# Two adaLN columns ahead of x, squares summed on TensorE, h from wide products, angles and softplus on GpSimd

## The chip, the core and the metric

The kernel runs on one core of a Trainium2 chip. The metric is the device time of one execution in microseconds (us); lower is better. TensorE (PE) multiplies matrices into PSUM; its weight loads stand apart as PEld. VectorE (DVE), ScalarE (ACT) and GpSimd (POOL) do the elementwise work, SyncE (SP) issues most of the transfers. Each engine takes its instructions from a queue of its own, in order, and waits on semaphores for the others.

## The reference

A decoder trunk of two layers on one sequence of 256 tokens, 1024 wide. Each layer modulates a normalised x by the condition c (adaLN), projects it once for three branches, and adds the gated merge to x. Cut to what matters here:

```python
c_act = jax.nn.silu(c)
mod = c_act @ ada_w + ada_b                      # 3072 columns a layer
shift, scale, gate = jnp.split(mod, 3, axis=-1)
h = rmsnorm(x, norm_g) * (1.0 + scale) + shift   # 256 x 1024
z = h @ w_in                                     # 1024 x 13312, split into:
# a_x, a_g | b_q, b_k, b_v, b_g | c_q, c_k, c_v, c_g | m_g
# A: u = causal_dwconv(a_x); log_a = -8 * sigmoid(..u..) * softplus(-lam); scan; * silu(a_g)
# B: q = rope(rmsnorm(b_q, qn_g), pos) / 8; k = rope(rmsnorm(b_k, kn_g), pos); attention; * silu(b_g)
# C: log_alpha from (h @ gla_a1) @ gla_a2; chunked linear attention; * silu(c_g)
x = x + gate * ((mg0 * (ya @ proj_a) + mg1 * (yb @ proj_b) + mg2 * (yc @ proj_c)) @ w_o)
```

`rope` turns q and k by the cosine and sine of the angle position times inverse frequency. Softplus of lam concerns 1024 numbers a layer, and only branch A's gates use it.

## The kernel before, in words

**Layout.** x lies with its 1024 features on 8 x 128 partitions and the 256 tokens along the free axis (`x_sb`, 128 x 8 x 256). All weights come as one stream (`ws`) in units, in an order fixed in the program. A unit is a piece of a projection: T units are 256 rows of the matrices q, k, v or bg with up to 512 columns (four of them make one matrix for one pair of heads), F units 128 columns over all 1024 rows (conv branch `ax`, its gate `ag`, and others). SyncE loads each unit into one of six `raw` buffers. Matmuls run in three products to keep f32 accuracy: ScalarE casts `raw` to `whi` (L232), VectorE takes the remainder `wlo` (L233), and TensorE adds hi·hi, lo·hi and hi·lo (L799 to L801 for q, k, v and others of their kind, L787 to L789 for bg, L807 to L809 for F units). There are four `whi` and four `wlo` buffers, and four PSUM buffers `mm`.

**adaLN.** c is activated, and `crow` is made of it by matmuls of ones with a diagonal (L318, L322): c's 1024 numbers along the free axis, on every partition. A column of the modulation is then one product with sum on VectorE (`ada_tile`, L334), over 1024 elements per partition. Layer 0 needs 16 columns, a scale and a shift for each of the 8 tiles of h; a scale is multiplied by the norm's weight (L336) and is then `mod`. The table `START` sets which columns stand ahead of which unit in the stream: four before unit 0, four before unit 4, and so on. The first ten are loaded into buffers that lie free at the start (`ada_yhi`, `ada_ylo`, `ada_hraw`, ...).

**The start.** SyncE issues c, the unit matrix, x in two halves, the vector of small parameters (`vec_sb`), and then the stream. `stats_start` squares x on ScalarE (L381, four instructions of 512 columns), adds the squares on VectorE (L384, L385), and sums over partitions by two matmuls with ones (L388). `rstd_full` turns this into 1/rms by ln and exp on ScalarE and one step of Newton's method on VectorE (L351 to L357). The casts of units 0 to 3 are put behind these steps by `tc.issue_after`.

**The first block.** Units 0 to 15 are q, k, v and bg of the first pair in four rounds. Between them stand the adaLN columns; with each shift column `h_tile` makes one tile of h: VectorE the product of x, `mod` and rstd (`tmp`, L366), ScalarE `hhi` (L368), VectorE `hlo` (L369). Hooks at units 2, 15 and 16 add `tables` (the angles in `angles`, their sine and cosine, and the tables `ctab` and `stab` that also hold the norm weights of q and k), loads of masks, and `small` (`softplus`, L399 to L410).

**The hand-over.** When a matrix is done, `evac_qk` squares it on ScalarE, makes two products with the tables on VectorE (`ra` L562, `rb` L564) and a sum of the squares (`ss` L566), adds the halves on GpSimd (`ro`, L567 and L568), and at its end scales `ss` and raises it to the power -1/2 on GpSimd (L569, L570). `gen_qk` multiplies `ro` by `ss` on VectorE (L575), and TensorE transposes the product (L177). q and k have two PSUM buffers each, one for each half of the tokens: q0, q1, k0, k1. The next units, the F units of the conv branch, take those buffers in turn; each of them is evacuated on VectorE by the steps of the convolution (`ya`, L887). `gen_la` runs in between: it splits the factor of the low-rank decay into `a_sb` (GpSimd, L479) and `t` (L466) and multiplies them on TensorE (L469, L485). bg's result becomes `sgb` (L858).

**What sets the order.** The program is written in the order of the dependences; a list scheduler with a time for each instruction sorts each engine's queue, and `tc.issue_after` puts an instruction behind another. A pool's buffer is waited for by whoever writes it next.

## Time and profile before

| | |
|---|---|
| three runs, us | 906.34, 906.39, 908.03 (median 906.39) |
| the profiled execution, us | 906.63, of which span 904.9 |
| TensorE busy | 865.6 us (96%), weight loads 818.7 (90%) |
| VectorE busy | 671.9 us (74%) |
| ScalarE busy | 531.8 us (59%) |
| GpSimd busy | 179.1 us (20%) |
| moved | 170.16 MB |

The span runs from the first instruction to the last of the profiled execution, and the device time holds a little around it. The shares are averages over stages that differ; the rows below take the first 100 us apart, where all that the change touches is done. In a timeline a row gives the start, the duration, the engine, the line, the operation, out<-in by the program's names with shape, and in brackets the idle time ahead of it and what ended it. Durations of neighbours can overlap, since an instruction begins while the one before it drains.

### The profile page before, as it was taken

Reading aid. Unit: us, or ns where it says so; the run is one execution under the profiler, and the core shown is the slowest. Engines: PE = TensorE matmul, PEld = TensorE weight load, DVE = VectorE, ACT = ScalarE, POOL = GpSimd, SP = SyncE. Lnnn points to the kernel's source line nnn. Section 1 sums busy time; section 2 is a strip of 40 time slices with the busy share of each in tenths; the row PEclk is TensorE's granted clock in tenths of the full one; section 3 lists DMA queues with packets and bytes.
Section 4 is the critical chain, followed back from the end, with each engine's and each line's share of the span. In section 5 each row is a group of like instructions: output and inputs, shape, how many; then the busy total and the mean of one; then the engine's idle time right before and its main releaser. Section 6 shows DMA issues by size and latency. Waiting matters only on the chain.

```text
span 904.9 us, 16407 instructions
## 1 busy us (share of the span) xinstructions
PE 865.6 (96%) x6340; PEld 818.7 (90%) x6340; DVE 671.9 (74%) x1115; ACT 531.8 (59%) x897; POOL 179.1 (20%) x160
## 2 busy tenths in 40 slices
PE   3989999999999999999999999989999999999998
PEld 2978999999988888998989999979999988899998
DVE  6998899669667667656776788986896666656674
ACT  4376976686544554644454689666874545554451
POOL 0026365224000110100030525651430001000000
PEclk7999999999999999999999999999999999999999
DMA  8884456446756666676654644553567455455651
GB/s 334 309 290 138 146 174 193 141 134 195 248 184 197 205 212 201 212 236 205 224 168 148 191 146 144 176 194 117 184 205 239 163 189 166 148 173 187 191 167 47
DMA packets 52111, 170.16 MB, mean 188 GB/s; under 512 B 6240, under 2 KB 8160, under 8 KB 52032
## 3 DMA queue, kind: packets, MB, share of 16 engines
q1 hardware_dynamic: 51216, 167.04, 56.8%
q10 hardware_dynamic: 672, 1.87, 0.7%
q8 instruction: 50, 0.82, 0.4%
q0 software_dynamic: 144, 0.20, 0.2%
q14 instruction: 29, 0.24, 0.1%
HBM read 168.23 MB, written 1.05 MB: 187 GB/s over the span
## 4 chain that ended last, share of the span: by engine, by line
PE 51%; DVE 19%; DMA 12%; issue 8%; ACT 5%; POOL 4%; DVEq 0%; SPq 0%; ACTq 0%
DMA raw<-in_ada_dram 10%; PE mm L807 10%; PE mm L809 10%; PE mm L808 10%; DVE wlo L233 8%; PE mm L799 5%; PE mm L800 5%; PE mm L801 4%; POOL ss L570 2%; PE xps L177 1%; ACT whi L232 1%; DVE raw L334 1%; DVE rb L564 1%; DMA g_raw<-in_gates_dram 1%; DVE ra L562 1%
## 5 line engine op out<-in xcount | busy, mean ns | idle before, releaser
L233 DVE TENSOR_TENSOR wlo<-raw,whi 128x1024 fp32r<-128x1024 f32 (+2 forms) x288 | 335.3, 1171 | 84.5 <-ACT whi L232 83.1
L232 ACT CAST whi<-raw 128x1024 fp32r<-128x1024 f32 (+2 forms) x288 | 280.1, 976 | 185.2 <-PE mm L808 120.4
L807 PE MATMUL mm<-hhi,whi 128*128 128x256 f32 x768 | 217.1, 283 | 2.9 <-DVE rb L564 2.9
L809 PE MATMUL mm<-hhi,wlo 128*128 128x256 f32 x768 | 216.0, 282 | 3.5 <-DVE wlo L233 3.5
L808 PE MATMUL mm<-hlo,whi 128*128 128x256 f32 x768 | 215.4, 280 | 0.0
L799 PE MATMUL mm<-whi,hhi 128*128 128x384 f32 (+2 forms) x480 | 169.5, 358 | 7.2 <-ACT hhi L368 6.5
L800 PE MATMUL mm<-wlo,hhi 128*128 128x384 f32 (+2 forms) x480 | 171.3, 358 | 1.6 <-DVE wlo L233 1.4
L801 PE MATMUL mm<-whi,hlo 128*128 128x384 f32 (+2 forms) x480 | 167.6, 355 | 0.5 <-DVE hlo L369 0.5
L807 PEld LDWEIGHTS mm<-hhi,whi 128*128 128x128 f32 x768 | 146.0, 190 | 4.5 <-ACT tmp L857 2.9
L809 PEld LDWEIGHTS mm<-hhi,wlo 128*128 128x128 f32 x768 | 145.6, 190 | 4.7 <-DVE wlo L233 4.1
L808 PEld LDWEIGHTS mm<-hlo,whi 128*128 128x128 f32 x768 | 145.7, 190 | 0.3
L799 PEld LDWEIGHTS mm<-whi,hhi 128*128 128x128 f32 x480 | 92.9, 195 | 14.5 <-ACT hhi L368 7.5
L800 PEld LDWEIGHTS mm<-wlo,hhi 128*128 128x128 f32 x480 | 93.4, 195 | 9.1 <-DVE wlo L233 3.2
L334 DVE CUSTOM_DVE_ANT_0 raw<-raw,crow,vec_sb 128x1024 f32<-128x1024 f32 x38 | 48.7, 1283 | 70.2 <-DMA raw<-in_ada_dram 70.2
L801 PEld LDWEIGHTS mm<-whi,hlo 128*128 128x128 f32 x480 | 92.5, 194 | 6.7 <-DVE hlo L369 0.8
L807 PE MATMUL mm<-yhi,whi 128*128 128x256 f32 x320 | 89.9, 281 | 1.5 <-DVE mg L949 1.5
L808 PE MATMUL mm<-ylo,whi 128*128 128x256 f32 x320 | 89.4, 279 | 0.0
L809 PE MATMUL mm<-yhi,wlo 128*128 128x256 f32 x320 | 89.2, 279 | 0.0
L807 PEld LDWEIGHTS mm<-yhi,whi 128*128 128x128 f32 x320 | 60.4, 189 | 2.5 <-DVE mg L949 1.7
L809 PEld LDWEIGHTS mm<-yhi,wlo 128*128 128x128 f32 x320 | 60.1, 188 | 0.8 <-DVE mod L334 0.4
L808 PEld LDWEIGHTS mm<-ylo,whi 128*128 128x128 f32 x320 | 60.1, 188 | 0.0
L708 POOL TENSOR_TENSOR at_hl<-att_sb,at_hl 128x384 fp32r<-128x384 f32 x8 | 8.8, 1096 | 206.3 <-ACT at_hl L707 206.3
(236 smaller groups left out, 1409.2 us busy)
## 6 DMA issues: line engine op xcount, KB each, us to landing
raw<-in_ws_dram SPq DMA_DIRECT2D x192, 512.0 KB, 4.2
raw<-in_ws_dram SPq DMA_DIRECT2D x88, 384.0 KB, 3.1
raw<-in_ada_dram SPq DMA_DIRECT2D x38, 512.0 KB, 4.5
raw<-in_ws_dram SPq DMA_DIRECT2D x8, 400.0 KB, 4.6
g_raw<-in_gates_dram ACTq DMA_DIRECT2D x3, 512.0 KB, 4.5
x_sb<-in_x_t_dram SPq DMA_DIRECT2D x2, 512.0 KB, 6.6
ada_yhi<-in_ada_dram SPq DMA_DIRECT2D x2, 512.0 KB, 7.8
ada_ylo<-in_ada_dram SPq DMA_DIRECT2D x2, 512.0 KB, 9.0
```

The costliest lines, as they stand in the source:

```text
L177: seen[0] = T.transpose(*a, **k).ins
L232: A.copy(hi, r)
L233: V.tensor_tensor(lo, r, hi.bitcast(F32), ALU.subtract)
L334: V.tensor_tensor_reduce(w, w, crow2, 1.0, b, ALU.mult, ALU.add, a if i == 0 else m)
L562: V.tensor_tensor(ra.rearrange("p (g s) d -> p g s d", g=3), z4, ctab[l][:, i, t].unsqueeze(2).to_broadcast(bc), ALU.mult)
L570: G.tensor_tensor(ss, ss, mhalf[:, 0:12].rearrange("p (a b) -> p a b", a=2), ALU.pow)
L799: T.matmul(o, ah, wh, start=(k == 0), stop=False)
L800: T.matmul(o, ah, wl, start=False, stop=False)
L801: T.matmul(o, al, wh, start=False, stop=(k == KT - 1))
L807: T.matmul(ps[:, 0:S], hi[:, a:b], xh[:, k], start=(k == 0), stop=False)
L808: T.matmul(ps[:, 0:S], hi[:, a:b], xl[:, k], start=False, stop=False)
L809: T.matmul(ps[:, 0:S], lo[:, a:b], xh[:, k], start=False, stop=(k == nk - 1))
```

## The change

- The first two adaLN columns are loaded ahead of x, and `vec_sb` on ScalarE's queue.
- At the start TensorE runs eight matmuls of ones by ones, two with the diagonal and, in `rstd_full`, three of `m`, whose results nobody reads. The squares are not added on VectorE any more: TensorE sums all eight tiles.
- h of layer 0 is made by `h_first`: VectorE multiplies x by rstd in wide pieces (`xr`, L382: 256, 256, 512 and 1024 columns), ScalarE applies scale and shift (`tmp`) and casts (`hhi`), VectorE takes the remainder (`hlo`, L393). The product of a scale with the norm's weight goes to ScalarE.
- The angles go to GpSimd but for the last limit, softplus to GpSimd but for one reciprocal, with Abs and Relu on ScalarE. In place of one fused step each, GpSimd takes two. The tables take four products in place of eight.
- The casts of units 0 to 3 are tied to other instructions, and `tables` no longer waits for the last `hlo`.

```diff
         if it in early:
...
+            if it[2] == 1:
+                for i in range(2):
+                    SY.dma_start(out=x_sb[:, 4 * i:4 * i + 4], in_=x_t[:, 4 * i:4 * i + 4])
...
                     if it[1] < 4:
-                        st.enter_context(tc.issue_after(cur["ra"]))
-                        st.enter_context(tc.issue_after(cur["rv"]))
+                        st.enter_context(tc.issue_after(cur["h0a" if it[1] else "ra"]))
                     A.copy(hi, r)
+                with ExitStack() as st:
+                    if it[1] < 4:
+                        st.enter_context(tc.issue_after(cur["xr0"]))
                     V.tensor_tensor(lo, r, hi.bitcast(F32), ALU.subtract)
...
+    A.dma_start(out=vec_sb, in_=vec)
     SY.dma_start(out=eye_sb, in_=eye)
-    for i in range(2):
-        SY.dma_start(out=x_sb[:, 4 * i:4 * i + 4], in_=x_t[:, 4 * i:4 * i + 4])
-    SY.dma_start(out=vec_sb, in_=vec)
...
+    warm_up(ones, 8)
...
+    warm_up(diag[:, 0:2].rearrange("p k n -> p (k n)"), 2)
...
         if i == 0:
-            V.tensor_tensor(m, a, vcol(l, V_NG + j), ALU.mult)
+            A.activation(m, a, AF.Copy, scale=vcol(l, V_NG + j))
         if l == 0 and i == 1:
-            h_tile(0, j, cur["rstd"], cur["h"])
+            h_first(j, cur["xr"], cur["h"])
...
+    def x_scaled(i, a, b):
...
+        v = V.tensor_tensor(cur["xr"][i][:, a:b], x_sb[:, 4 * i + a:4 * i + b],
+                            cur["rstd"].unsqueeze(1).to_broadcast([P, b - a, S]), ALU.mult)
+        cur.setdefault("xr0", v.ins)
+    def h_first(j, xr, h):
+        if j in (1, 2, 4):
+            x_scaled(j // 4, j % 4, 2 if j == 1 else 4)
+        hi, lo, f = h[0], h[1], tmp()
+        A.activation(f, xr[j // 4][:, j % 4], AF.Identity, bias=mod[:, 0, 1, j:j + 1], scale=mod[:, 0, 0, j:j + 1])
+        a = A.copy(hi[:, j], f)
+        cur.setdefault("h0a", a.ins)
+        v = V.tensor_tensor(lo[:, j], f, hi[:, j].bitcast(F32), ALU.subtract)
...
-            if i % 2:
-                V.tensor_tensor(sq[i - 1], sq[i - 1], t, ALU.add)
-        V.tensor_tensor(sq[0], sq[0], sq[2], ALU.add)
         ps = xps()
-        for j in range(2):
-            T.matmul(ps[:, 0:S], ones, sq[0][:, j], start=(j == 0), stop=(j == 1))
+        for j in range(KT):
+            T.matmul(ps[:, 0:S], ones, sq[j // 2][:, j % 2], start=(j == 0), stop=(j == KT - 1))
...
-        V.scalar_tensor_tensor(e, lam, -1.0, lam, ALU.mult, ALU.max)
+        A.activation(e, lam, AF.Abs)
         A.activation(e, e, AF.Exp, scale=-1.0)
-        V.tensor_scalar(s, e, 2.0, None, ALU.add)
+        G.tensor_scalar(s, e, 2.0, None, ALU.add)
         V.reciprocal(s, s)
-        V.tensor_tensor(s, s, e, ALU.mult)
-        V.tensor_tensor(s2, s, s, ALU.mult)
-        V.tensor_scalar(p, s2, 1.0 / 17.0, None, ALU.mult)
-        for k in range(7, 0, -1):
-            V.scalar_tensor_tensor(p, p, 1.0 / (2 * k + 1), s2, ALU.add, ALU.mult)
...
+        G.tensor_tensor(s, s, e, ALU.mult)
+        G.tensor_tensor(s2, s, s, ALU.mult)
+        G.tensor_scalar(p, s2, 1.0 / 17.0, 1.0 / 15.0, ALU.mult, ALU.add)
+        for k in range(6, -1, -1):
+            G.tensor_tensor(p, p, s2, ALU.mult)
+            G.tensor_scalar(p, p, 1.0 / (2 * k + 1), None, ALU.add)
+        G.tensor_tensor(p, p, s, ALU.mult)
+        A.activation(e, lam, AF.Relu, scale=-1.0)
...
         for c in (c1, c2, c3):
-            V.scalar_tensor_tensor(an, k, -c, an, ALU.mult, ALU.add)
+            G.tensor_scalar(kc, k, -c, None, ALU.mult)
+            G.tensor_tensor(an, an, kc, ALU.add)
         lim = 3.1415925
         V.tensor_scalar(an, an, lim, -lim, ALU.min, ALU.max)
...
-    rstd = rstd_full(sts)
+    rstd = rstd_full(sts, 3)
+    cur["rstd"], cur["xr"] = rstd, {}
+    x_scaled(0, 0, 1)
...
         a, v = cur["h_last"]
-        with tc.issue_after(a), tc.issue_after(v):
+        with tc.issue_after(a):
             load_after(("sy", "a", 3), (pos_sb, pos), (inv_sb, inv.partition_broadcast(P)))
```

The lines move by up to 27 behind the edits: L564 is then L589, L570 is L595, L575 is L600, L807 is L832. How the queues change at three places:

VectorE at the start, before: two of the column reductions (L334, which stand as two rows each) lie between the steps of rstd (L351 to L357).

```order
L336 TENSOR_TENSOR mod<-acc,vec_sb 128x1
L351 TENSOR_SCALAR rs_m<-xps 128x256
L334 ISA ada_ylo,acc<-ada_ylo,crow,vec_sb 128x1024
L334 ISA acc 128x1
L355 TENSOR_TENSOR rs_q<-rs_y 128x256
L334 ISA ada_ylo,mod<-ada_ylo,crow,vec_sb 128x1024
L334 ISA mod 128x1
L336 TENSOR_TENSOR mod<-acc,vec_sb 128x1
L356 TENSOR_TENSOR rs_q<-rs_q,rs_m 128x256
L357 SCALAR_TENSOR_TENSOR rs_y<-rs_q,rs_y 128x256
L233 TENSOR_TENSOR wlo<-raw,whi 128x800
```

VectorE at the start, now:

```order
L340 ISA ada_ylo,acc<-ada_ylo,crow,vec_sb 128x1024
L340 ISA acc 128x1
L340 ISA ada_ylo,mod<-ada_ylo,crow,vec_sb 128x1024
L340 ISA mod 128x1
L357 TENSOR_SCALAR rs_m<-xps 128x256
L361 TENSOR_TENSOR rs_q<-rs_y 128x256
L362 TENSOR_TENSOR rs_q<-rs_q,rs_m 128x256
L363 SCALAR_TENSOR_TENSOR rs_y<-rs_q,rs_y 128x256
L382 TENSOR_TENSOR xr<-x_sb,rs_y 128x256 x2
L238 TENSOR_TENSOR wlo<-raw,whi 128x800
```

All four reductions of the first columns now stand ahead of rstd's steps, which follow each other, and the first two products of x and rstd (`xr`) come before the first remainder.

GpSimd at the hand-over, before, from `a_sb` to the power of q (`mhalf` is the exponent; the first two `ro` are of q0, the next two of q1):

```order
L479 TENSOR_TENSOR a_sb<-a_raw,a_sb 16x512
L567 TENSOR_TENSOR ro<-ra,rb 128x6x32
L568 TENSOR_TENSOR ro<-ra,rb 128x6x32
L466 TENSOR_TENSOR t_631<-t_606,t3r 128x2x16
L567 TENSOR_TENSOR ro<-ra,rb 128x6x32
L568 TENSOR_TENSOR ro<-ra,rb 128x6x32
L569 TENSOR_SCALAR ss<-ss 128x12
L570 TENSOR_TENSOR ss<-ss,mhalf 128x12
```

GpSimd at the same place, now, the last steps of softplus (`spl`, `sp`, `sp4n`) up to the power of q; 15 more steps of softplus, q0's two `ro` and `t` stand between `a_sb` and the first of these rows:

```order
L428 TENSOR_TENSOR spl_819<-spl_819,spl_818 128x16
L429 TENSOR_SCALAR spl_819<-spl_819 128x16
L430 TENSOR_TENSOR spl_819<-spl_819,spl_817 128x16
L432 TENSOR_SCALAR spl_819<-spl_819 128x16
L433 TENSOR_TENSOR spl_819<-spl_819,spl_816 128x16
L434 TENSOR_SCALAR sp_169<-spl_819 128x16
L435 TENSOR_SCALAR sp4n<-spl_819 128x16
L592 TENSOR_TENSOR ro<-ra,rb 128x6x32
L593 TENSOR_TENSOR ro<-ra,rb 128x6x32
L594 TENSOR_SCALAR ss<-ss 128x12
L595 TENSOR_TENSOR ss<-ss,mhalf 128x12
```

All of softplus on GpSimd now stands ahead of q1's `ro`, the scaling of `ss` and the power.

VectorE at the hand-over, before, from k0's evacuation (`ra`, `rb`, `ss`) to k1's; `spl` are steps of softplus:

```order
L562 TENSOR_TENSOR ra<-mm,ctab 128x384
L564 TENSOR_TENSOR rb<-mm,stab 128x384
L566 TENSOR_REDUCE ss<-sqq 128x6
L887 SCALAR_TENSOR_TENSOR ya<-mm,vec_sb,ya 128x254
L408 SCALAR_TENSOR_TENSOR spl_794<-spl_794,spl_793 128x16
L858 SCALAR_TENSOR_TENSOR sgb<-tmp,xps 128x256
L575 TENSOR_TENSOR ro<-ro,ss 128x768
L887 SCALAR_TENSOR_TENSOR ya<-mm,vec_sb,ya 128x253
L410 SCALAR_TENSOR_TENSOR spl_794<-spl_794,spl_791 128x16
L562 TENSOR_TENSOR ra<-mm,ctab 128x384
L564 TENSOR_TENSOR rb<-mm,stab 128x384
L566 TENSOR_REDUCE ss<-sqq 128x6
```

VectorE at the same place, now:

```order
L587 TENSOR_TENSOR ra<-mm,ctab 128x384
L589 TENSOR_TENSOR rb<-mm,stab 128x384
L591 TENSOR_REDUCE ss<-sqq 128x6
L883 SCALAR_TENSOR_TENSOR sgb<-tmp,xps 128x256 x2
L912 SCALAR_TENSOR_TENSOR ya<-mm,vec_sb,ya 128x254
L238 TENSOR_TENSOR wlo<-raw,whi 128x1024
L600 TENSOR_TENSOR ro<-ro,ss 128x768
L587 TENSOR_TENSOR ra<-mm,ctab 128x384
L589 TENSOR_TENSOR rb<-mm,stab 128x384
L591 TENSOR_REDUCE ss<-sqq 128x6
```

The steps of softplus are gone here, a remainder stands ahead of the product of `ro` and `ss`, and k1's evacuation still follows that product.

TensorE where the fourth F unit begins, before (the last products of the third, L485 and the transposes, the first of the fourth):

```order
L807 MATMUL mm<-hhi,whi 128x256
L808 MATMUL mm<-hlo,whi 128x256
L809 MATMUL mm<-hhi,wlo 128x256
L485 MATMUL xps<-t1t,a_sb 128x256 x2
L177 MATMUL xps<-eye_sb,ro 128x128 x3
L807 MATMUL mm<-hhi,whi 128x256
L808 MATMUL mm<-hlo,whi 128x256
L809 MATMUL mm<-hhi,wlo 128x256
```

TensorE at the same place, now:

```order
L834 MATMUL mm<-hhi,wlo 128x256
L832 MATMUL mm<-hhi,whi 128x256
L510 MATMUL xps<-t1t,a_sb 128x256 x2
L833 MATMUL mm<-hlo,whi 128x256
L834 MATMUL mm<-hhi,wlo 128x256
L832 MATMUL mm<-hhi,whi 128x256
L833 MATMUL mm<-hlo,whi 128x256
L834 MATMUL mm<-hhi,wlo 128x256
L832 MATMUL mm<-hhi,whi 128x256
L833 MATMUL mm<-hlo,whi 128x256
L177 MATMUL xps<-eye_sb,ro 128x128 x3
```

The product with `a_sb` (now L510) and the first transposes (L177) come behind the first products of the fourth unit.

## Rows read from the trace of the kernel before

**Rows 1.** Busy time by stretch: length, PE, PEld, DVE, ACT, POOL, PEclk, DMA share, GB/s.

```profile
20.30:62.00 41.70, 40.33 (x240) 38.38 (x240) 41.37 (x91) 20.45 (x31) 2.89 (x1) 0.95 0.90 329
...
74.00:97.00 23.00, 22.69 (x185) 21.52 (x184) 18.82 (x33) 18.62 (x32) 9.61 (x9) 1.00 0.38 110
```

**Rows 2.** Start: timeline; landing of ada_yhi; busy PE and PEclk of a stretch.

```profile
3.05 1.38 SPq L199 DMA_DIRECT2D ada_yhi<-in_ada_dram  x2
...
DMA to landing us min/median/max: 7.5/7.8/8.1
...
4.59 3.47 PE L322 MATMUL xps<-diag,ones 128*128 128x128 f32 x16 [4.59 <-DVE diag L318]
...
7.95 2.27 ACT L381 ACTIVATE sq<-x_sb 128x512 f32<-128x512 f32 x4 [5.32 <-DMA x_sb<-in_x_t_dram]
...
11.80:13.90 2.10, 2.05 (x4) 0.50 1.02 413
...
18.02 0.42 DVE L357 SCALAR_TENSOR_TENSOR rs_y<-rs_q,rs_y 128x256 f32<-128x256 f32 x1
...
20.34 0.70 PE L799 MATMUL mm<-whi,hhi 128*128 128x400 f32 x1 [6.47 <-ACT hhi L368]
```

**Rows 3.** VectorE's groups from 20 to 62: busy us, mean ns of one.

```profile
L369 DVE SCALAR_TENSOR_TENSOR hlo<-tmp,mod,hhi 128x256 fp32r<-128x256 f32 x8 | 4.8, 607 | 0.0
L366 DVE SCALAR_TENSOR_TENSOR tmp<-x_sb,mod,rs_y 128x256 f32<-128x256 f32 x7 | 3.4, 479 | 0.0
...
L431 DVE SCALAR_TENSOR_TENSOR an<-an 128x64 f32<-128x64 f32 x3 | 0.7, 218 | 0.0
```

**Rows 4.** Timeline at the end of the first block.

```profile
56.14 1.28 ACT L400 ACT_TABLE_LOAD   x1
56.26 2.89 POOL L479 TENSOR_TENSOR a_sb<-a_raw,a_sb 16x512 fp32r<-16x512 f32 x1 [54.27 <-ACT a_sb L478]
56.80 1.22 DVE L233 TENSOR_TENSOR wlo<-raw,whi 128x1024 fp32r<-128x1024 f32 x1
...
57.93 1.50 DVE L369 SCALAR_TENSOR_TENSOR hlo<-tmp,mod,hhi 128x256 fp32r<-128x256 f32 x1
```

**Rows 5.** GpSimd's timeline; then line L569 over the whole span: ns min/median/max.

```profile
62.73 1.66 POOL L568 TENSOR_TENSOR ro<-ra,rb 128x192 f32<-128x192 f32 x1
...
71.98 2.30 POOL L570 TENSOR_TENSOR ss<-ss,mhalf 128x12 f32<-128x12 f32 x1
...
140.69 0.60 POOL L568 TENSOR_TENSOR ro<-ra,rb 128x192 f32<-128x192 f32 x1
...
372.17 1.49 POOL L479 TENSOR_TENSOR a_sb<-a_raw,a_sb 16x512 fp32r<-16x512 f32 x1 [4.49 <-issue]
...
508.16 0.25 POOL L466 TENSOR_TENSOR t<-t,t3r 128x32 f32<-128x32 f32 x1
...
L569 POOL TENSOR_SCALAR ss<-ss x16: 200/969/1262, 71.7 to 664.5; 128x12 f32<-128x12 f32 x16
```

**Rows 6.** TensorE at the hand-over: timeline, and busy time with PEclk by stretch.

```profile
69.47 0.55 PE L807 MATMUL mm<-hhi,whi 128*128 128x256 f32 x1 [2.69 <-DVE rb L564]
...
69.40:72.40 3.00, 2.93 (x14) 0.50 0.72 229
72.40:73.80 1.40, 1.40 (x13) 0.99 0.70 248
...
76.75 0.50 PE L485 MATMUL xps<-t1t,a_sb 48*128 48x256 f32 x2
...
77.49 0.37 PE L807 MATMUL mm<-hhi,whi 128*128 128x256 f32 x1
```

**Rows 7.** VectorE at the hand-over: timeline; the group of sgb from 59 to 75.

```profile
61.02 0.55 DVE L562 TENSOR_TENSOR ra<-mm,ctab 128x384 f32<-128x384 f32 x1
...
74.42 1.26 DVE L575 TENSOR_TENSOR ro<-ro,ss 128x768 f32<-128x768 f32 x1
...
L858 DVE SCALAR_TENSOR_TENSOR sgb<-tmp,xps 128x256 f32<-128x256 f32 x4 | 1.5, 405 | 0.0
```

More of the change, by code (lines that the diff above doesn't have):

```diff
@@ L370, in h_tile @@
         cur["h_last"] = (a.ins, v.ins)
+    def x_scaled(i, a, b):
+        if a == 0:
+            cur["xr"][i] = one.tile([P, 4, S], F32, name="xr", tag=("pt1", "pt0")[i])
+        v = V.tensor_tensor(cur["xr"][i][:, a:b], x_sb[:, 4 * i + a:4 * i + b],
[9 more added lines that the diff above has]
+        v = V.tensor_tensor(lo[:, j], f, hi[:, j].bitcast(F32), ALU.subtract)
+        cur["h_last"] = (a.ins, v.ins)
     def square_x(j):
@@ L429, in angles @@
         c3 = float(2 * np.pi - c1 - c2)
+        kc = two.tile([P, 2, 32], F32, name="an", tag="ro")
         for c in (c1, c2, c3):
-            V.scalar_tensor_tensor(an, k, -c, an, ALU.mult, ALU.add)
+            G.tensor_scalar(kc, k, -c, None, ALU.mult)
+            G.tensor_tensor(an, an, kc, ALU.add)
         lim = 3.1415925
@@ L977, in small @@
             softplus()
-        V.tensor_scalar(vec_sb[:, :, V_ON:V_ON + 2], vec_sb[:, :, V_ON:V_ON + 2], 0.5, None, ALU.mult)
+        G.tensor_scalar(vec_sb[:, :, V_ON:V_ON + 2], vec_sb[:, :, V_ON:V_ON + 2], 0.5, None, ALU.mult)
     sts = layer(0, h, {2: tables, 15: load_small, 16: small})
```

42 lines of the change are left out of this document (21 added, 21 removed).

## The prediction

> **What bounds the kernel now.** I read the page first, then the busy time by stage, then the timeline of the stages that the change touches, and last the waits at their ends. The span is 904.9 us. The stages tell more than its averages: from 20.3 to 62 VectorE is busy 41.37 of 41.7 us, and from 74 to 97 TensorE is busy 22.69 of 23 [rows 1]. So the first input block (q, k, v and bg of the first pair, with the adaLN columns between) is paced by VectorE and by the buffers that it frees. From 74 on TensorE runs nearly without a gap, so a microsecond lost or won before that point stays to the end, unless something behind it has slack of its own. The order of the instructions from about TensorE's 760th row on (some 165 us) is that of before, so I look for no effect there.
>
> Three stages stand ahead of that point: the start (first weighted matmul at 20.34 [rows 2]), the block, and the hand-over, in which VectorE frees TensorE's four PSUM buffers (q0, q1, k0, k1) one after the other for the first matrices of the conv branch; I call these F1 to F4. TensorE starts F2 at 69.47, when q1 is free, after 2.69 us of idling, and F4 at 77.49 [rows 6].
>
> **The start.** The two columns put ahead of x cost x their place. Loads in that place (ada_yhi now) are issued at 3.05 and land 7.5 to 8.1 us later, so x lands at about 10.6 and 11.9, where its first half is now used at 7.95 [rows 2]. The four squarings (2.27 us) so end at 13.1. The three additions of squares leave VectorE, and TensorE gets eight matmuls in place of two, which stand as four records and took 2.05 us at a granted clock of 0.50, which is 1.2 GHz [rows 2]. Sixteen records of 128 columns, for crow, took 3.47 us mostly at that level [rows 2]; the eight are sixteen of 256 columns, 6.9 us from 11.2 on, or they trail the squares at twice the rate: their end lies between 14.9 and 18.4 (6.9 from 11.2, and some 0.3 for the last), against 13.87. Behind it VectorE no longer runs two column reductions before the last step of rstd (18.02 [rows 2]): ln, exp, three steps of VectorE, two products and two steps of ScalarE are left, nine steps, some 4 us by the last step's 0.42. That makes the first weighted matmul 18.9 to 22.4. I take 20.6, the clock rising half way: +0.3, with ends of -1.4 and +2.1. The warm-up matmuls lie in idle time and cost nothing else; the load of vec_sb on ScalarE's queue and hb on GpSimd have nobody waiting.
>
> **The block.** A row's duration holds some 0.08 us in which the next one has begun (56.80 + 1.22 against 57.93 [rows 4]), so I take that off. VectorE loses eight tmp products at 0.40 (3.2 us), and eight products of one column, which go to ScalarE, and eleven steps of the angles at 0.14 or less (0.218 less 0.08 at 64 columns), 2.0 [rows 3]; it gains the products of x and rstd, 2048 columns in four instructions, 2.4 us by the cast of 1024 in 1.14 (1.22 less 0.08 [rows 4]). The eight table products become four of twice the width: nothing. Net: -2.8. Today's last hlo took 1.50 us, where its like take 0.48 (4.8 less 1.5, over the seven others [rows 3]), because GpSimd's a_sb held it up [rows 4]; in the new order a_sb comes behind it: -1.0. So VectorE's block, which ends at 59.4, ends at 55.9 by this sum with the start's +0.3, and at 56.8 if the last weights, whose buffers come free hardly earlier than now, are what it waits for. ScalarE has room for its second step per h tile (20.45 busy of 41.7 [rows 1]). GpSimd's angle chain (twelve small steps) starts when positions land and VectorE needs it some 8 us later; a step there waits for the VectorE instruction that is running, and at worst VectorE waits out the rest of the chain, 2 us.
>
> **The hand-over, where it is decided.** Softplus goes from VectorE to GpSimd as 23 small steps, each waiting for the one before. Nobody needs the result soon, but GpSimd's queue is in order, and behind it stand the four ro additions of q and the power of ss. VectorE's product of ro and ss waits for that power; behind this product, on VectorE's in-order queue, stands the evacuation of k1; and for k1's buffer TensorE waits with F4.
> - GpSimd starts late. The exp behind the table load (1.28 [rows 4]) follows the last cast of ScalarE, which ends where VectorE's last cast begins, 54.8 to 55.7. So the exp is done at 56.3 to 57.2, then a_sb's cast (about 0.6), and a_sb takes 1.49 us undisturbed [rows 5]: the first multiply of softplus begins at 58.5 to 59.4. ScalarE's Relu waits for that multiply too, with the first squares of q behind it, so VectorE evacuates q0 from about 60.3, where it now does at 61.02 [rows 7].
> - GpSimd's queue from there to the end of the power: 22 steps of softplus at 0.28 (0.20 for 12 columns, and 0.08 to the next, dependent one: from 71.70 to 71.98), 6.2 us; four ro additions, 2.4; t, 0.3; the scaling of ss, 0.3; the power, 2.3 [rows 5]. Sum 11.5: it would end at 70.0 to 70.9 undisturbed.
> - It is disturbed. ro took 0.60 us beside an instruction that reads PSUM and 1.66 us beside a cast of VectorE: it waited for the cast to end [rows 5]. Six casts of 1.14 stand in that stretch, 6.8 us, in which GpSimd gets about one step (0.35) through per cast: 4.7 us more. The power ends at 74.7 to 75.6; I take 75.5, the late end, since one GpSimd step can also miss a gap.
> - VectorE reaches the product after three evacuations (three steps of 0.55 less 0.08 each: 1.4), six casts (6.8), three sgb and two conv steps at 0.33 to 0.4 (1.8) [rows 7]: 60.3 + 12.8 = 73.1. It then waits 2.4 us. Now it does not wait: the power ended at 74.28 and the product began at 74.42.
> - The product takes 1.18 less its overlap, say 1.1, the two halves of k1 0.47 each: F4 starts at 77.6, where it now starts at 77.49. But L485 and L177, 0.7 us, which TensorE has now done ahead of F4 (76.75 [rows 6]), come behind it. Shift: 77.6 + 0.7 - 77.5 = +0.8.
> - TensorE has finished F3 by 73.2 (its buffer is free at 70.5) and idles 4.4 us. After the idling of 2.69 the granted clock was 0.50 from 69.4 to 72.4, where 14 matmuls took 3.0 us; 13 took 1.40 right after, at 0.99 [rows 6]. So some 1.5 us were lost at the low level, and I count the same behind the longer idling.
>
> Sum: +0.8 + 1.5 = **+2.3 us**. The profiled execution took 906.63, the median of the runs is 906.39, so its own offset is small: 906.4 + 2.3 = **908.7**. What the first two stages gain does not show in this sum except through the exp, which opens GpSimd's chain.
>
> A rule against the change. The trace shows GpSimd's two-input step of 32 columns at 0.25 us undisturbed [rows 5], against 0.22 for VectorE's at 64 columns [rows 3]. The Trainium skill, GPSIMD Engine Reference, section 4.1 (Engine selection), sends elementwise work to VectorE, since GpSimd is about twice as slow with two inputs. An estimate by that factor would make eleven of the steps 0.36 instead of 0.25 and the time 1.2 us longer, 909.9; the row at this size stands against the factor, so the sum keeps 0.25 and less.
>
> **Rivals.**
> - GpSimd in time. If its small steps slip in between VectorE's instructions, the power ends by 71 and VectorE's own queue sets F4: 73.1 + 2.0 = 75.1, shift 75.1 + 0.7 - 77.5 = -1.7; TensorE then idles only 1.9 us, less than the 2.69 after which the clock fell, so nothing is added: 904.7. If TensorE is also at the high level from its early work on, so that the start is 1.4 earlier, 903.3. For it: steps of 0.20 are seen. Against it: 11 of the 16 scalings of ss were stretched (median 0.97), as the row of ro next to a cast is. The Trainium skill, TensorE: Matmul & The Clock Gate, Part 1, says that the halved clock is the default and that activity lifts it; by that rule the early matmuls would give this rival's start, while the trace has no stretch that shows the clock through the idling before x lands.
> - One of the two. GpSimd late but the clock held, or GpSimd in time and the clock fallen: 906.2 to 907.2, no difference that can be told.
> - Much slower. One place, GpSimd's queue: if the low clock holds through all eight square matmuls (start +2.1) and steps miss two VectorE instructions each, the power ends past 78 and TensorE waits as long: 911 to 912.5. It decides against the kernel from the point where the power ends later than 74.7.
> - That the change doesn't do what it says: the clock at the squares stays low in spite of the warm-up. It is in the start's bounds, and GpSimd's chain hides most of it.
>
> **How the numbers follow.** A measurement of this kernel can tell about 0.2%, 1.8 us: below 904.6 is faster, above 908.2 slower. The forecast has 0.36, with 907.7 to 910.5 as its own range; much slower 0.09; one of the two 0.31; GpSimd in time with the gain of the start, 0.24. So faster 0.24, same 0.31, slower 0.45. The range runs from 903.6 to 911.2 and leaves out the ends of the first rival and of the last.
>
> **What would show it.** Right: in the chain of waits VectorE's product of ro and ss (L600) waits 1 to 4 us for the power of GpSimd (L595), TensorE waits 3 to 5 us for rb at F4, and the granted clock falls after it; GpSimd is busy almost throughout from 58 to 76. The first weighted matmul stands within 2 us of 20.34, and VectorE's last hlo of the block at 55 to 57. Wrong: L600 starts without a wait before 74, or TensorE is at F4 by 75.5; then the time is 905 or less. A start past 22 or an angle chain that VectorE waits for over 2 us would make it slower for another reason.

## The result, and the profile after

The changed kernel is slower: 913.29 us (median of 7 runs, 909.8 to 919.5) against 907.99 for the kernel before on the same chips, a ratio of 1.0076, 95% interval 1.0052 to 1.0101. A second measurement, beside the experiments, gave 1.0068 (1.0049 to 1.0086). The prediction had +2.3 us, with 911.2 as its upper end; the profiled execution took 913.29 where that of before took 906.63, 6.7 us more. The direction and the place were right, the size was not.

Busy time by stretch, with the columns of [rows 1]:

```profile
20.30:62.00 41.70, 38.24 (x229) 36.09 (x228) 35.67 (x57) 24.69 (x46) 12.90 (x23) 0.96 0.89 324
62.00:74.00 12.00, 9.73 (x81) 9.29 (x79) 11.53 (x17) 8.36 (x20) 10.86 (x19) 1.00 0.61 203
74.00:97.00 23.00, 18.06 (x115) 17.16 (x114) 13.00 (x21) 11.80 (x22) 10.32 (x11) 0.78 0.24 72
```

VectorE has 5.7 us less to do in the block (35.67 against 41.37), and it wins nothing: from 74 to 97 TensorE, 22.69 us busy before, is 18.06 busy, at a mean clock of 0.78.

The start's timeline (it answers [rows 2]), then the busy time by stretch, with the columns of [rows 1], while TensorE sums the squares:

```profile
9.70 1.15 ACT L405 ACTIVATE sq<-x_sb 128x512 f32<-128x512 f32 x2 [1.62 <-DMA x_sb<-in_x_t_dram]
...
10.38 3.72 PE L409 MATMUL xps<-sq,ones 128*128 128x256 f32 x16 [2.06 <-ACT sq L405]
...
18.38 0.46 PE L824 MATMUL mm<-whi,hhi 128*128 128x400 f32 x1 [1.60 <-ACT hhi L391]
...
10.30:14.10 3.80, 3.71 (x16) 2.96 (x16) 2.15 (x5) 2.15 (x6) 0.00 (x0) 1.00 1.03 420
```

x lands later than before, as the prediction had it, but the eight matmuls of squares (sixteen records) run at the high level, at a granted clock of 1.00, and the first weighted matmul comes 1.96 us earlier than before. That is this trace; in the second one of the same kernel it comes at 21.1 (see below).

The angles in the block, a timeline of VectorE and TensorE, and the busy time by stretch (all engines) behind it:

```profile
37.49 0.20 DVE L458 TENSOR_SCALAR an<-an 128x64 f32<-128x64 f32 x1 [1.94 <-POOL an L456]
...
42.26 1.85 DVE L238 TENSOR_TENSOR wlo<-raw,whi 128x800 fp32r<-128x800 f32 x2
...
43.29 0.53 PE L825 MATMUL mm<-wlo,hhi 128*128 128x400 f32 x1 [2.43 <-DVE wlo L238]
...
43.50:46.90 3.40, 3.40 (x11) 3.37 (x11) 3.40 (x7) 1.24 (x2) 0.00 (x0) 0.50 0.77 249
```

VectorE waits 1.94 us for GpSimd's angles, the four table products follow, two remainders come behind those, and TensorE, which waits for the first of them, idles 2.43 us. Its granted clock is 0.50 (1.2 GHz) for the next 3.4 us. In the block of before the longest gap is 0.70 us.

The hand-over, from the timelines of ScalarE, GpSimd, VectorE and TensorE (it answers [rows 5 to 7]), then TensorE's busy time and clock:

```profile
59.34 0.22 ACT L431 ACTIVATE spl<-vec_sb 128x16 f32<-128x16 f32 x1 [1.75 <-POOL spl L424]
60.15 0.56 DVE L587 TENSOR_TENSOR ra<-mm,ctab 128x384 f32<-128x384 f32 x1 [2.44 <-ACT sqq L582]
61.27 0.22 POOL L428 TENSOR_TENSOR spl<-spl,spl 128x16 f32<-128x16 f32 x1
61.57 1.30 POOL L429 TENSOR_SCALAR spl<-spl 128x16 f32<-128x16 f32 x1
...
71.57 0.25 POOL L435 TENSOR_SCALAR sp4n<-spl 128x16 f32<-128x16 f32 x1
...
74.39 2.31 POOL L595 TENSOR_TENSOR ss<-ss,mhalf 128x12 f32<-128x12 f32 x1
76.73 1.34 DVE L600 TENSOR_TENSOR ro<-ro,ss 128x768 f32<-128x768 f32 x1 [3.17 <-POOL ss L595]
78.47 0.54 DVE L589 TENSOR_TENSOR rb<-mm,stab 128x384 f32<-128x384 f32 x1
79.16 0.55 PE L832 MATMUL mm<-hhi,whi 128*128 128x256 f32 x1 [4.94 <-DVE rb L589]
...
77.66:87.90 10.24, 8.74 (x38) 0.50 0.13 38
87.90:92.00 4.10, 4.10 (x34) 1.00 0.29 96
```

This is the predicted chain, step by step: softplus on GpSimd ends at 71.8, the power at 76.70, VectorE's product waits 3.17 us for it, k1's evacuation follows, and F4 starts at 79.16 after 4.94 us of idling. Then TensorE runs at half its clock for 8.74 busy us, where the prediction counted on 3.

### The profile page after: what moved, and what is told of

Its sections match the earlier page's. It is cut to its first block, busy times and chain, and to the rows that moved or that the text cites. A ratio compares the mean times of both kernels' runs of the same rounds, so it can differ in the third digit from the quotient of the medians.

```text
span 911.5 us, 16507 instructions
## 1 busy us (share of the span) xinstructions
PE 875.0 (96%) x6378; PEld 825.6 (91%) x6378; DVE 664.6 (73%) x1055; ACT 538.6 (59%) x924; POOL 196.2 (22%) x197
## 4 chain that ended last, share of the span: by engine, by line
PE 53%; DMA 16%; DVE 14%; issue 7%; POOL 5%; ACT 4%; SPq 0%; DVEq 0%; ACTq 0%; POOLq 0%
DMA raw<-in_ada_dram 12%; PE mm L832 9%; PE mm L834 9%; PE mm L833 9%; DVE wlo L238 7%; PE mm L825 5%; PE mm L826 5%; PE mm L824 5%; PE xps L177 2%; POOL ss L595 2%; ACT whi L234 1%; DMA inv_sb<-in_inv_dram 1%; DMA ada_hraw<-in_ada_dram 1%; PE ps_s L173 1%; PE xps L173 1%
## 5 line engine op out<-in xcount | busy, mean ns | idle before, releaser
L832 PE MATMUL mm<-hhi,whi 128*128 128x256 f32 x768 | 217.1, 283 | 7.2 <-DVE rb L589 7.2
L832 PEld LDWEIGHTS mm<-hhi,whi 128*128 128x128 f32 x768 | 145.9, 190 | 9.1 <-issue 5.2
L832 PE MATMUL mm<-yhi,whi 128*128 128x256 f32 x320 | 90.1, 282 | 1.7 <-DVE mg L974 1.7
L832 PEld LDWEIGHTS mm<-yhi,whi 128*128 128x128 f32 x320 | 60.3, 189 | 2.7 <-DVE mg L974 1.9
```

The lines of the kernel that those rows point to most:

```text
L832: T.matmul(ps[:, 0:S], hi[:, a:b], xh[:, k], start=(k == 0), stop=False)
```

## The experiments

Each kernel was timed against the kernel before on its own chip. The times spread over 4 to 12 us between executions, so effects are read from the ratios, and mechanisms from the traces, of which there is one for each row. q0's evacuation is the first `ra` on VectorE. Where it begins differs between traces of one kernel (60.15 and 63.05 in the two of after), and F4 moves with it; the last column is the time from it to F4, 16.47 us in the kernel before.

| kernel | median us | ratio to before (95%) | F4 starts | idle ahead of it | q0 to F4 |
|---|---|---|---|---|---|
| after | 913.29 | 1.0076 (1.0052 to 1.0101) | 79.16 | 4.94 | 19.01 |
| after, again | 915.33 | 1.0068 (1.0049 to 1.0086) | 82.06 | 5.06 | 19.01 |
| after, x first | 914.98 | 1.0064 (1.0048 to 1.0080) | 80.19 | 4.19 | 18.52 |
| softplus on VectorE | 909.47 | 1.0027 (1.0009 to 1.0046) | 78.55 | 1.68 | 16.63 |
| angles on VectorE | 910.98 | 1.0042 (1.0012 to 1.0071) | 80.48 | 4.51 | 18.61 |
| both on VectorE | 907.57 | 1.0002 (0.9983 to 1.0021) | 77.05 | 1.43 | 16.71 |
| softplus late on GpSimd | 907.71 | 1.0007 (0.9989 to 1.0025) | 78.55 | 1.58 | 16.30 |
| TensorE kept busy | 910.05 | 1.0032 (1.0012 to 1.0051) | 81.13 | 0.68 | 19.03 |
| q's generator held | 908.34 | 1.0021 (0.9997 to 1.0044) | 79.67 | 4.29 | 18.66 |
| held, product behind k1 | 904.94 | 0.9973 (0.9959 to 0.9988) | 76.97 | 0.36 | 14.79 |
| the same, angles on VectorE | 900.99 | 0.9929 (0.9906 to 0.9952) | 77.15 | 0.40 | 14.48 |
| the same, angles on VectorE, more warm-up | 901.45 | 0.9936 (0.9915 to 0.9957) | 73.25 | 0.69 | 14.66 |
| the same, both on VectorE | 900.07 | 0.9921 (0.9902 to 0.9941) | 75.19 | none | 16.57 |
| before, softplus on GpSimd | 909.07 | 1.0019 (1.0002 to 1.0037) | 77.52 | 3.33 | 17.52 |
| before, angles on GpSimd | 906.37 | 0.9995 (0.9976 to 1.0015) | 77.43 | 1.23 | 14.98 |
| before, product behind k1 | 906.52 | 0.9987 (0.9967 to 1.0007) | 76.29 | none | 15.17 |

**Softplus back on VectorE** with the fused steps of before, all else as in after.

```diff
-        G.tensor_scalar(s, e, 2.0, None, ALU.add)
+        V.tensor_scalar(s, e, 2.0, None, ALU.add)
         V.reciprocal(s, s)
-        G.tensor_tensor(s, s, e, ALU.mult)
+        V.tensor_tensor(s, s, e, ALU.mult)
...
```

> The kernel after with softplus as before, in fused steps on VectorE; all else stays. Theory (queue): in the trace of after the power of q (L595) begins at 74.39, behind the 22 steps of softplus on GpSimd, and F4 starts at 79.16. Without these steps the power begins as soon as the two ro additions of q1 are done, VectorE's product of ro and ss does not wait, F4 starts at 75 or before, TensorE idles under 2.7 us there and the granted clock stays at 1.00 from 75 to 90. Time 904 to 906.5, 0.1 to 0.5% under before. Rival (start or block): if the columns ahead of x or the wide products are what costs, F4 still starts behind 78 and the time stays over 911.

VectorE's product no longer waits, the clock stays up, and from q0's evacuation to F4 it takes 16.63 us instead of 19.01, so the mechanism at the hand-over holds; about 0.45% is won back. But the rest of the expectation missed: the kernel is still slower than before, and F4 starts at 78.55, since q0's evacuation begins at 61.92 in this trace, between the two times that the kernel after itself shows. What is left pointed to the block, and to the angles.

**Softplus on GpSimd, behind the last power of k** (`cur["pow"]`).

```diff
-        with tc.issue_after(a), tc.issue_after(v):
+        with tc.issue_after(cur["pow"]):
             softplus()
```

> The kernel after with all steps of softplus put behind the power of k on GpSimd; they stay on GpSimd. Theory (place in the queue): F4 starts at 75 or before, as with softplus on VectorE, no idle stretch of TensorE over 2.7 us and a granted clock of 1.00 from 75 to 90; 903 to 906. Rival (GpSimd itself): if GpSimd is so slowed by VectorE's instructions that the four ro additions and the power alone end behind 76, F4 starts behind 78 and the time stays over 911. Second rival: the late softplus delays the tanh of the gates of branch A, and the loss reappears between 95 and 110.

At least as much is won by changing only its place in GpSimd's queue: it is not GpSimd that costs but who stands behind it. F4 misses 75 for the same reason (q0's evacuation at 62.25). TensorE has no gap of over 0.25 us between 95 and 110, so the second rival fell.

**TensorE kept busy while it waits**, with five matmuls into a buffer that nobody reads.

```diff
+                if i == 19:
+                    wps = pss.tile([P, 512], F32, name="ps_s", tag="s")
+                    with tc.issue_after(cur["f3"]):
+                        for _ in range(5):
+                            T.matmul(wps, ones, crow2[:, 0:512], start=True, stop=True)
```

> The kernel after with five matmuls of 512 columns, whose result nobody reads, on TensorE between F3 and F4 (some 4.3 us); the wait of F4 for k1's evacuation stays. Theory (the clock is a cost of its own): F4 starts at 79.2 to 79.6 as in after, but the granted clock is 1.00 from 77.7 to 87.9, where it was 0.50 and TensorE 8.74 us busy: 4.4 us are won, 908.5 to 909.5. Rival (the wait alone costs, and the clock is made up for by slack behind it): no change, 913.

TensorE by stretch:

```profile
73.00:91.00 18.00, 17.32 (x114) 1.00 0.30 85
```

F4 comes no earlier (81.13, later than expected since q0's evacuation begins at 62.10), yet 0.36 to 0.44% of the time is back. The clock behind the wait is a cost of its own, and by these numbers the larger part: the next pair puts the wait and the clock together at 0.48%. Each of these differences is known to some 0.3% only.

**The product behind k1's evacuation**, and **the control** for it. Holding q's generator until k's also reorders what stands behind F4, so the control holds it too (until unit 13), but lacks the last two of the diff's added lines and leaves the product ahead of k1's evacuation.

```diff
+                        if i == 12:
+                            held = gen_qk(l, nm, p, ro, ss)
...
+            if (l, nm, p) == (0, "q", 0):
+                es.enter_context(tc.issue_after(cur["rb", 0, "k", 0]))
             V.tensor_tensor(ro, ro, ss.unsqueeze(3).to_broadcast([P, 2, 6, 64]), ALU.mult)
```

> The kernel after with VectorE's product of ro and ss of q (L600) put behind the evacuation of k1; softplus stays ahead of the power on GpSimd. Theory (VectorE's in-order queue carries the wait): the power still ends near 76.7, but k1's evacuation waits only for the buffer that q1's ro additions free at 74.0, rb ends at 75.1 and F4 starts there; TensorE idles 1 to 1.5 us, the clock stays at 1.00: 905 to 907.5. Rival (F4 is held by something else that comes with a busy GpSimd): F4 still starts behind 78, over 911.

> The control for the run with the product behind k1: the kernel after, in which q's generator is handed over one unit later, together with k's, as there, but VectorE's product of ro and ss is not tied to k1's evacuation and stands ahead of it again. This changes the order of the instructions behind F4 (from about 100 to 440) as in that run, and leaves the hand-over as in after. Theory: F4 starts at 78.5 to 80 behind the power of q, the clock falls behind it, and the run is 3 to 6 us over the 904.94 of the run with the product behind k1: 908 to 911. Rival (what was won there comes from the order behind F4 alone): 904 to 906.

VectorE and TensorE, first the product behind k1, from its trace:

```profile
78.38 1.35 DVE L603 TENSOR_TENSOR ro<-ro,ss 128x768 f32<-128x768 f32 x1 [1.10 <-POOL ss L595]
...
76.97 0.36 PE L835 MATMUL mm<-hhi,whi 128*128 128x256 f32 x1 [0.36 <-DVE rb L589]
...
75.00:90.00 15.00, 13.58 (x109) 1.00 0.28 78
```

and the control:

```profile
77.26 1.34 DVE L602 TENSOR_TENSOR ro<-ro,ss 128x768 f32<-128x768 f32 x1 [2.49 <-POOL ss L595]
...
79.67 0.55 PE L834 MATMUL mm<-hhi,whi 128*128 128x256 f32 x1 [4.29 <-DVE rb L589]
...
78.30:92.00 13.70, 12.33 (x53) 0.50 0.21 59
```

In the first the product still waits for the power, but nobody waits for the product, and q0's evacuation is followed by F4 after 14.79 us instead of 18.66. The two differ by 0.48% (1.0021 against 0.9973), some 4.4 us. This is the most direct sign that VectorE's in-order queue carries GpSimd's delay to TensorE. It is not quite clean: TensorE's order still differs in places up to about its 685th row, and the control's trace, with the longest low clock of all, is of the slowest of its eleven executions (914.78). F4 came 1.9 us later than the 75.1 expected for the first (q0's evacuation at 62.18). The control itself is 0.47% under after again; the order behind F4 that comes with the holding is the known difference, but what it is worth isn't taken apart here.

**The angles back on VectorE**, softplus still early on GpSimd; **both back**; and **the angles alone moved in the kernel before**.

```diff
-            G.tensor_scalar(kc, k, -c, None, ALU.mult)
-            G.tensor_tensor(an, an, kc, ALU.add)
+            V.scalar_tensor_tensor(an, k, -c, an, ALU.mult, ALU.add)
...
```

> The kernel after with the angles as before, in fused steps on VectorE; softplus stays on GpSimd ahead of the power. What led to it: in all runs with the angles on GpSimd VectorE waits for them 1.9 to 2.4 us at some 35 to 38, the four table products come ahead of two remainders, and TensorE idles 2.4 us at 41 to 45, after which the granted clock is 0.50 for 3.4 to 6.8 us. Theory (two faults, one behind the other): that idling and the low clock at 43 to 47 go, but q0's evacuation still waits for ScalarE's Relu, which waits for GpSimd, so it begins at 59.5 to 60.5 and F4 still waits for the power of q and starts at 78 to 79.5: 910 to 913. Rival (the angles are the whole fault): F4 starts at 76 or before, under 908.

> The kernel after with both, the angles and softplus, as before on VectorE: what is left is the new start (columns ahead of x, squares on TensorE, warm-up) and h from wide products. Theory: TensorE does not idle over 1 us between 20 and 60, its clock is 1.00 there, q0's evacuation begins 1 to 3 us before that of the kernel before (61.02), F4 starts at 74.5 to 76.5, 903 to 905.5: faster than before by 0.2 to 0.4%. Rival (the new start and the wide products win nothing that lasts, since the transfers set the block's end): q0's evacuation at 60.5 to 62 and 906.5 to 908.5.

> The kernel before with the angles alone on GpSimd as in after. Theory: VectorE waits for the chain 1 to 3 us, the eight table products come ahead of two remainders, TensorE idles 1.5 to 3 us at 40 to 47 and its clock falls to 0.50 for 3.4 us behind it; q0's evacuation moves from 61.02 to 62.5 to 64.5, and the whole kernel is 1.5 to 4 us slower than before, 908.5 to 911. Rival (the wait is made up for before the block ends, since VectorE has eleven steps less): q0's evacuation at 60.5 to 61.5, 906 to 907.5.

With the angles on VectorE TensorE's idling at 41 to 45 and the low clock behind it are gone, and F4 still waits for the power: two faults, one behind the other, as expected (only q0's evacuation, at 61.87, and F4, at 80.48, come later than expected). With both back the time is that of before, so the new start and the wide products together win nothing that lasts. The two faults about add up: taken back alone the angles are worth 0.26 to 0.34%, softplus 0.41 to 0.49%, both together 0.66 to 0.74%. The expectation of a gain fell: q0's evacuation does come earlier, at 60.34, but of that 0.7 us F4 keeps 0.4 (77.05 against 77.49), and between 130 and 147 TensorE idles three times for remainders and `ro`, 1.95 us in all, where before it was 0.2. The same three stand in after, at 136.6 to 152.9. The last of the three, in the timeline of both back (its trace is of the slowest of its ten executions, 910.38):

```profile
146.82 0.45 PE L821 MATMUL mm<-wlo,hhi 128*128 128x384 f32 x1 [1.04 <-DVE wlo L238]
```

The kernel before with the angles moved has the whole damage in the block,

```profile
39.00 0.20 DVE L435 TENSOR_SCALAR an<-an 128x64 f32<-128x64 f32 x1 [1.94 <-POOL an L433]
...
45.18 0.46 PE L802 MATMUL mm<-wlo,hhi 128*128 128x400 f32 x1 [3.00 <-DVE wlo L233]
```

and yet its time is that of before, the rival's, though not by the rival's way (q0's evacuation begins at 62.45, as the theory had it). Its hand-over takes the delay up. From F1 to F4, here and then in before, all engines with the columns of [rows 1]:

```profile
65.90:77.40 11.50, 9.36 (x78) 8.85 (x77) 11.50 (x22) 8.09 (x16) 8.22 (x6) 1.00 0.69 198
```

```profile
62.20:77.50 15.30, 11.27 (x80) 10.63 (x80) 15.30 (x32) 10.05 (x22) 10.95 (x11) 0.89 0.46 150
```

F1 starts at 65.95 instead of 62.19, 3.8 us later, and F4 at the same time. Half of that comes back as idling: TensorE idles only 2.1 us from there to F4, where before it idled 4.0 (2.69 of them in [rows 6]). The rest is mostly the clock, which stays at 1.00 here, and about the same matmuls take 9.36 us instead of 11.27.

**Softplus alone moved in the kernel before.**

> The kernel before with softplus alone on GpSimd as in after. Theory: GpSimd's 22 steps start behind a_sb at 59 to 60, the power of q ends at 76.5 to 78.5 (74.28 in before), VectorE's product waits for it 2 to 4 us, F4 starts at 78.5 to 80.5 behind 4 to 6 us of idling, and the clock is 0.50 behind it for 3.4 us or longer: 910 to 913, 0.3 to 0.6% over before. Rival (VectorE's sixteen steps less win as much as the wait costs): 906.5 to 908.5.

The product waits 3.48 us for the power and the clock is 0.50 for 6.8 us, but with its shorter queue VectorE is earlier there, and F4 starts as before (77.52). The loss is 0.19%, between the expectation (0.3 to 0.6%) and its rival: in the trace, moved alone, softplus costs nearly only the clock.

**After once more, and after with x ahead of the columns.**

```diff
-            if it[2] == 1:
-                for i in range(2):
-                    SY.dma_start(out=x_sb[:, 4 * i:4 * i + 4], in_=x_t[:, 4 * i:4 * i + 4])
...
     SY.dma_start(out=eye_sb, in_=eye)
+    for i in range(2):
+        SY.dma_start(out=x_sb[:, 4 * i:4 * i + 4], in_=x_t[:, 4 * i:4 * i + 4])
```

> The kernel after itself once more, beside the two others of this call. Theory: F4 starts at 78.5 to 80.5 behind 4 to 5 us of idling of TensorE, and the clock behind it is 0.50 for 3.4 to 13.7 us, by the execution, which costs 1.5 to 6 us: the runs spread over 7 us or more, with their median at 0.5 to 0.9% over before. Rival (the low stretch of 10.2 us in the first trace was an exception): a low stretch of 3.4 us, a spread under 5 us, and under 0.5%.

> The kernel after with x loaded ahead of the first two adaLN columns, as in before; all else stays. Theory (the start's gain is lost further on): the first weighted matmul moves from 18.38 to 19.5 to 21, q0's evacuation stays within 1 us of 60.15, since GpSimd's softplus lets ScalarE go on and not TensorE, F4 starts at 78.5 to 80.5, and the time is that of after within 1.5 us. Rival (the start passes through to the end): 1.5 to 2.5 us over after.

The loss repeats; the five runs spread over 3.8 us, less than expected, and F4 came at 82.06, later than expected. The first weighted matmul came at 21.1 in this trace of after and at 20.77 with x first, so the traces don't show that the order of these loads moves the start. The two times differ by 0.04% (914.98 and 915.33), less than their intervals: it doesn't reach the end.

**What a better kernel takes from this**: the product behind k1 with the angles, and with both, on VectorE; the first of these with more warm-up; and the edit alone in the kernel before.

> The run with VectorE's product behind k1's evacuation, and the angles on VectorE besides; softplus stays on GpSimd ahead of the power. Theory: no idling of TensorE at 41 to 45 and no low clock behind it; q0's evacuation begins at 59.5 to 60.5 (Relu waits for GpSimd), 2 us before that of the run it is made from (62.18); F4 starts at 75 to 76 (76.97 there): 903 to 904.5, 0.5 to 1.5 us less than the 904.94 of that run. Rival (F4 is bound by the ro additions of q1, which stand behind softplus on GpSimd, and these do not move): F4 at 76.5 to 77.5, 904.5 to 906.

> The angles and softplus on VectorE as before, and the product of ro and ss behind k1's evacuation: the fastest run so far (softplus on GpSimd, 900.99) but with softplus back on VectorE. It tells whether softplus on GpSimd wins anything once nobody waits for it. Theory (VectorE paces the hand-over, so each of its steps counts): sixteen steps of 0.16 to 0.4 us stand between 59 and 76 on VectorE, F4 starts 0.5 to 1.5 us later than there (77.15), 901.5 to 903.5. Rival (it wins nothing): 900 to 901.5.

> The run with the angles on VectorE and the product late, with six instead of two matmuls of the diagonal ahead of the squares (some 1.7 us more, in the stretch from 8.3 to 10.4 in which TensorE idles before x lands). In the runs so far the start comes in two kinds: first weighted matmul at 18.4 to 18.7 where the clock is 1.00 from its rise at some 6 on, and at 20.4 to 21.0 where it is 0.50 from 11 to 13 on for 3.4 us. Theory (the idling before x decides which): the clock stays at 1.00 until the block, first weighted matmul at 18.3 to 18.9; with that the block ends 0 to 2 us earlier, 899 to 901. Rival (the idling has no part in it): first weighted matmul at 20.4 to 21.0, 901 to 902.

> The kernel before with the edit of the run with the product behind k1 (q's generator handed over with k's, the product of ro and ss behind k1's evacuation), and nothing of the change. Theory: here the product does not wait, so k1's evacuation gains at most the product's 1.2 us; the new order behind F4 is worth what it is worth in the other runs: 903 to 905.5. Rival (the order behind F4 is worth nothing by itself): 906 to 908.

The run with the angles on VectorE and the product late missed both of its ranges: F4, at 77.15, is the rival's, and the time, 900.99, lies under both. The fastest, 900.07 us, is 0.79% under the kernel before and some 1.5% under after, and it has nothing of the change on GpSimd: softplus there wins nothing once nobody waits for it (900.99 with, 900.07 without). Against both back (1.0002) F4 comes 1.9 us earlier, and most of the gain comes behind it, where the order is new. TensorE by stretch, both back and then with the product late, from the same number of matmuls on to the same number:

```profile
170.00:474.00 304.00, 294.85 (x2258) 1.00 0.64 199
```

```profile
166.00:464.00 298.00, 293.20 (x2257) 1.00 0.65 203
```

It idles 9.2 us there in the one and 4.8 in the other. Why the same order wins next to nothing in the kernel before (0.9987) stays open.

More warm-up kept the clock at 1.00 from some 9 to 60, as expected, but the first weighted matmul came at 19.63, not at 18.3 to 18.9, and the time, 901.45, is the rival's. In the trace the gain is there at F4 (73.25, 3.9 us before that of the run it is made from) and is lost behind it. Its TensorE and VectorE, then the busy time from F4 on, in it and in the run it is made from:

```profile
75.62 1.35 DVE L601 TENSOR_TENSOR ro<-ro,ss 128x768 f32<-128x768 f32 x1 [2.05 <-POOL ss L593]
...
85.69 0.38 PE L833 MATMUL mm<-hhi,whi 128*128 128x256 f32 x1 [1.20 <-DVE sga L925]
...
73.25:100.00 26.75, 24.18 (x184) 22.43 (x185) 20.59 (x35) 18.68 (x36) 14.43 (x11) 1.00 0.38 114
```

```profile
77.15:101.00 23.85, 23.78 (x184) 22.36 (x185) 20.46 (x35) 19.17 (x35) 11.59 (x10) 1.00 0.45 130
```

VectorE's product, which stands behind k1's evacuation, waits again for GpSimd's power, later units wait for VectorE, and TensorE idles 2.6 us where it idled 0.1. In the trace with both on VectorE, where q0's evacuation begins at the same time (58.62 against 58.59), the power ends at 71.17 instead of 75.58. So once F4 comes early enough, softplus ahead of the power is paid behind it. This rests on one trace of each.

## Why the prediction was wrong

**Right in its mechanism.** The chain of waits, its engines and its order are those of the prediction, and taking the product behind k1 shows what they cost, 0.48%, the larger part of what after loses. VectorE's last remainder of the block ends at 56.81 (56.8 as the later of the two cases), q0's evacuation begins at 60.15 (60.3), for the reason given, Relu's wait for GpSimd. That these two times agree is partly luck: the start came 2.2 us earlier than the forecast's 20.6 and the block lost about as much to the angles; in the second trace of after the evacuation begins at 63.05. The product waits 3.17 us (2.4), TensorE 4.94 (4.4). Of the rivals the one on GpSimd in time fell. The one called much slower (911 to 912.5) is nearest to the time, but in the first trace neither of its conditions held (a start 2.1 us later, a power that ends past 78); in the second the power ended at 79.61, moved by the later q0.

**Mis-sized: the clock behind F4.** The step "I count the same behind the longer idling" took 1.5 us from [rows 6]. In the trace of after the 0.50 lasted 10.24 us, 8.74 of them busy; half of that, 4.4 us, is what the low level cost. That is 2.9 us more, the largest miss of the sum. It is not a constant either; TensorE's stretches behind F4, in after again, with the angles on VectorE, and before with softplus on GpSimd:

```profile
79.80:86.60 6.80, 4.54 (x20) 0.50 0.15 30
```

```profile
80.20:83.60 3.40, 3.12 (x15) 0.51 0.40 120
```

```profile
77.30:84.10 6.80, 6.58 (x28) 0.50 0.32 87
```

With the 12.33 busy us of the control, and 9.11 with x first, the term is an estimated 1.6 to 6.2 us, half of the busy time in each of six traces. The prediction took 1.5, under the smallest of these, from the one instance in its trace, and gave it no range.

**Mis-sized: the power.** It ended at 76.70, 1.2 us behind the 75.5 of the sum and outside its 74.7 to 75.6, and F4 at 79.16 instead of 77.6. Most steps of softplus took 0.31 us from start to start, not 0.28, and three of the four `ro` took 1.41, 1.58 and 1.58 beside remainders of VectorE (the prediction's casts of VectorE). (Of the sixteen scalings of `ss` twelve, not eleven, were stretched.) So the sum with measured terms is 79.16 - 77.49 + 0.7 + 4.4 = 6.8 us, against the 6.7 of the two profiled executions. That the two agree so closely is partly luck, as the last paragraph of this section shows. The Trainium skill, SBUF — State Buffer, section "SBUF: two separate sides", calls the ports that VectorE and GpSimd share an exclusive lock, for a whole instruction, to whichever starts first, among others where VectorE has two inputs in SBUF. The rows of after agree: L429 took 1.30 us at 61.57, beside the remainder (two inputs, `raw` and `whi`) that begins at 61.55, and 0.25 at 60.28, where VectorE read PSUM.

**Overlooked: who waits for VectorE while it waits.** The prediction priced GpSimd's angle chain at "at worst ... 2 us" of VectorE, which is what it waited (1.94), and put nothing of it into the sum, without a reason. But the table products behind that wait stand ahead of two remainders, and those feed TensorE: 2.43 us of idling and an estimated 1.7 us of low clock (half of 3.40 busy). [rows 1] had TensorE 40.33 of 41.7 us busy in the block, some 4.3 of them at the low level (to 24.65), so TensorE was a pacer there beside VectorE, and the work taken from VectorE could not shorten it much; that last step is argued, not tested. The angles cost after some 0.25 to 0.44% by the three pairs of runs with and without them.

**Overlooked: the start has two kinds.** It was placed half way between a low and a high clock. The traces show one or the other: the first weighted matmul at 18.38 to 18.68 where the clock held, and at 20.4 to 21.1 where it fell at some 11 to 12.6 for 3.4 us (19.4 to 19.6 in three more that held it). No run shows that it reaches the end.

**Wrong: what is lost or won before 74 "stays to the end", and "no effect" from the 760th row on.** TensorE's order is the same from there on but for a few instructions, yet the distance between two executions changes behind it (the prediction allowed for slack there, and put no size to it). One row at some 165 us, in before, in after, in before with softplus on GpSimd, and in both back:

```profile
163.24 0.52 PE L177 MATMUL xps<-eye_sb,ro 128*128 128x128 f32 x3 [1.23 <-DVE sgb L634]
```

```profile
171.03 0.52 PE L177 MATMUL xps<-eye_sb,ro 128*128 128x128 f32 x3 [1.35 <-DVE sgb L659]
```

```profile
165.98 0.52 PE L177 MATMUL xps<-eye_sb,ro 128*128 128x128 f32 x3 [1.24 <-DVE sgb L636]
```

```profile
164.92 0.52 PE L177 MATMUL xps<-eye_sb,ro 128*128 128x128 f32 x3 [1.35 <-DVE sgb L655]
```

After is 7.8 us behind before there, 1.0 more than the sum, and 6.7 at the end. Softplus in before is 2.7 us behind there and 0.2 at the end. Both back, 0.4 us ahead at F4, is 1.7 behind there, since the order between differs: the unbroken run of TensorE that the prediction counted on is only in before. Part of what comes back is the clock again. TensorE's busy time and clock show two low stretches in before, of which after has only the second:

```profile
420.60:424.00 3.40, 3.40 (x16) 0.50 1.00 290
471.80:475.20 3.40, 3.40 (x9) 0.50 0.33 112
```

```profile
477.02:480.43 3.41, 3.41 (x9) 0.50 0.37 115
```

The rest stays open.

## What to carry to other kernels

Before moving small steps to an engine with a short queue, list what stands behind them there, and follow each wait through the in-order queues of the others up to the engine that sets the time; if a place behind the last waiter exists, put them there. Price an idle stretch of TensorE as the wait plus a low clock behind it, with a range from several instances, since one trace shows one length. And read the next stage, its idle time and its clock, before charging a delay or counting a gain: before's hand-over took up a delay of 3.8 us from the block, while with more warm-up a gain of 3.9 us at F4 was lost again, much of it to waits for GpSimd's powers.
